# Where weight blocks and streamed tiles start in SBUF: bytes left free at the head of five pools

## The chip, the cores and the metric

The kernel runs on one core of a Trainium2 chip. The metric is the device time of one execution in microseconds; three runs of the kernel before took 2027.7, 2025.62 and 2027.94 us, a median of 2027.7.

## The reference, cut to what matters

Two transformer blocks over one sequence of 512 tokens, 1024 wide, in float32. The first block is a feed-forward layer, a mixer (attention of three kinds beside a state-space layer), a second feed-forward layer and a gate. The second block has two layers, each a recurrent branch beside an mLSTM branch, with a projection in and a projection out. Almost all of the arithmetic is in products of a weight matrix with the activations:

```python
def swiglu(x, w1, w3, w2):
    return (jax.nn.silu(x @ w1) * (x @ w3)) @ w2
...
    h = h + 0.5 * swiglu(rmsnorm(h, norm_ffn1[i]), ffn1_w1[i], ffn1_w3[i], ffn1_w2[i])
    z = rmsnorm(h, norm_mix[i]) @ w_in[i]
...
    h = h + jnp.concatenate([o_nsa, o_s5], axis=-1) @ w_out[i]
    h = h + 0.5 * swiglu(rmsnorm(h, norm_ffn2[i]), ffn2_w1[i], ffn2_w3[i], ffn2_w2[i])
    gate = jax.nn.sigmoid(rmsnorm(h, norm_ple[i]) @ w_ple_gate[i])
...
    for l in range(DEPTH_2):
        h = rms_norm(x, norm_g[l]) * (1.0 + scale[:, None, :]) + shift[:, None, :]
        u = h @ w_in[l]
...
        y = jnp.concatenate([y_rg, y_ml], axis=-1) @ w_out[l]
```

## The kernel before

**Tiling.** Activations lie feature-major: a tile is 128 features (the partitions) by 512 tokens, 2048 bytes in each partition. A weight matrix is cut into blocks of 128 x 128, 512 bytes in each partition. Both are split into two parts of type float32r, a high and a low one, and `mm3` (L111) makes a product of three instructions: high weights with the high tile (L115), high weights with the low tile (L116), low weights with the high tile (L117). In each the weight block is the operand that is loaded into TensorE beforehand, and the tile of 512 tokens is streamed past it. For one output tile `mm3` runs over all blocks of a column of the weight matrix and adds up in one PSUM bank; two banks (pa and pb in the tiles' names, followed by the stage) take turns.

**Weights.** `Stream` (L46) brings the blocks in the order of their use, eight to a chunk of 4096 bytes in each partition: one DMA into a tile of the pool `wst` (L71), a copy on ScalarE that makes the high part `whi` (L86) and a subtraction on VectorE that makes the low part `wlo` (L88). Two chunks are loaded and two split ahead of use.

**Streamed tiles.** xnh and xnl, the parts of a layer's normed input, lie in the pool `xp` of 26 tiles. gh and gl, the inputs of a feed-forward layer's second product, lie in the pool `ffn` that `swiglu` opens (L254); xch, rxh, yrh, ymh and their low parts in the pool of a layer of the second block (`layer`, L1400), apart from yrl, which lies in `xp`; oh, ol, sh, sl in `mix2`, some oh and ol in `xp`; pp, the gate's second input, in `ple`.

**Order.** The order of the instructions of each engine is the order in which the program issues them; nothing is rescheduled.

**Places.** A pool gets a stretch of every partition's bytes and lays its tiles one behind the other. The pools at the bottom (`const`, `wst`, `whi`, `wlo`, `work`, `xp`) stay for the whole program; those of the stages are opened and closed above them. The pool `const` ends at byte 20192, which is 224 past a multiple of 512, so all weight blocks and the tiles of `xp` begin at such places. A stage's pool begins wherever the one under it ends.

Of the kernel before, what the change touches and what calls it, by code (L numbers as in the profile page):

```python
# [44 lines left out]

class Stream:  # L46
    """Weight blocks of 128 x 128 in the order of their use, eight to a chunk, each chunk
    loaded ahead and split into two float32r parts."""
# [12 lines left out]
    def release(self):  # L61
        """Go on with the splits that were held back."""
        self.hold = False
        self.split(self.pos // CH + 1 + self.SPLIT)
# [34 lines left out]
    def get(self, *blocks):  # L99
        """The next blocks (name, slicer, row, column), side by side."""  # L100
        n = len(blocks)
        c, r = divmod(self.pos, CH)
        assert r + n <= CH
        self.split(c + 1 + (0 if self.hold else self.SPLIT if r >= CH // 2 else self.SPLIT - 1))
        self.order += list(blocks)
        self.pos += n
        s = slice(r * 128, (r + n) * 128)
        return self.hi[c][:, s], self.lo[c][:, s]


def mm3(k, ps, w, x, start, stop):  # L111
    """ps += (w_hi + w_lo).T @ (x_hi + x_lo), all but the product of the low parts,
    which lies under the last bit."""
    mm = k.nc.tensor.matmul
    mm(ps, w[0], x[0], start=start, stop=False)  # L115
    mm(ps, w[0], x[1], start=False, stop=False)  # L116
    mm(ps, w[1], x[0], start=False, stop=stop)  # L117


class Norm:  # L120
    """Sums of squares of a feature-major tensor, gathered tile by tile, and the reciprocal
    root in both layouts."""
# [7 lines left out]
    def add(self, src, scale=1.0):  # L130
        """Two sums, one to an engine, put together at the end; where the end is waited for,
        the last tile stays by itself."""
# [25 lines left out]
    def early(self, eps=1e-6):  # L158
        """The mean but for the last tile."""
        k = self.k  # L160
        self.head = k.work.tile([128, 4], F32, name="nhead", bufs=2)
        k.nc.vector.tensor_scalar(self.head, self.colsums(self.acc[0]), 1.0 / DM, eps, op0=OP.mult, op1=OP.add)
# [29 lines left out]
def rsqrt(k, out, ms):  # L192
    """out = ms ** -0.5 by Newton steps from the exponent's half."""
# [14 lines left out]
def split_scaled(k, src, g):  # L208
    """The two float32r parts of src * g (g one value to a partition)."""
# [19 lines left out]
class Fill:  # L229
    """Work to be laid into the gaps that the matrix products leave to the other engines."""  # L230
# [23 lines left out]
def swiglu(k, xs, norm, w1, w3, w2, parts, on_tile, rate, at):  # L254
    """h += 0.5 * swiglu of the input whose parts are xs; norm is still to be finished."""
    nc = k.nc
    f0 = 0
    with k.tc.tile_pool(name="ffn", bufs=2) as pool:
        for hf, n in enumerate(parts):
# [50 lines left out]
def sincos(k, pool, phi, shape, name, sign=1.0):  # L310
    """Sine (with a sign) and cosine of an angle of any size: steps to be run in order, and a dict that
    gets the tiles "s" and "c"."""
# [26 lines left out]
def s5_prepare(k, pool, ins, scr):  # L339
    """Steps that lay the state-space layer's matrices into DRAM scratch."""  # L340
# [255 lines left out]
def rope(k, ps, out, b, scale, done, todo):  # L596
    """The halves of each head changed over in b; the rest with the steps that follow."""
# [13 lines left out]
def gelu(k, y, out, w, todo=None):  # L611
    """Twice the tanh form, which the reference has; w is room to work in."""
# [24 lines left out]
def mixer(k, xs, norm, ins, scr, on_tile):  # L637
    nc, v = k.nc, k.nc.vector
    with ExitStack() as outer:
# [137 lines left out]
        def step(b):  # L777
            """The outputs of one block of groups."""
# [7 lines left out]
        def keys(b):  # L786
            """The keys of each group twice over the partitions, high parts; the low parts once."""
# [10 lines left out]
        # the compressed keys and values  # L798
        KV = {}

        def cmp_blocks(x):
            """The tokens of each block, by the parity of the token, with the positions added."""
# [48 lines left out]
        def cmp_k(g):  # L851
            """The keys of the two groups, each on its own partitions and columns."""
# [8 lines left out]
        def cmp_v(g):  # L861
            """The values under each of a tile's two heads of both groups, apart from the other's."""
# [12 lines left out]
        # the order of the projections  # L875
# [87 lines left out]
        p2 = outer.enter_context(k.tc.tile_pool(name="mix2", bufs=1))  # L963

        k.phase = "att"

        # the compressed branch's weights, all heads and tokens
# [48 lines left out]
        # the two branches that see every earlier token  # L1016
        oT, op, qs = {}, {}, {}

        def att_q(j):
            """The high parts of a head's queries and the low parts, on the partitions one above the other."""  # L1020
# [10 lines left out]
        def att_s(u, g):  # L1031
            """Scores and their weights."""
# [19 lines left out]
        def att_d(u, g):  # L1052
            """The gate over the weights' sum on a diagonal."""
# [8 lines left out]
        def put(u, g, ps, at, t, kb):  # L1062
            """The weights on the tokens of one tile of keys, scaled, with the keys on the partitions."""
# [39 lines left out]
        # the gate of the state-space layer  # L1103
# [46 lines left out]
def log1p_small(k, pool, e, out, shape, name):  # L1150
    """ln(1 + e) for 0 <= e <= 1: twice the inverse hyperbolic tangent of e / (2 + e)."""
# [13 lines left out]
def second_prepare(k, pool, ins):  # L1165
    """Steps: what the two later layers take from their vectors alone."""
# [13 lines left out]
    for l in range(2):  # L1180
# [34 lines left out]
        def colsum(n, L=L, box=box):  # L1215
            """Eight of the columns' sums."""
# [112 lines left out]
def modulate(k, l, norm, gg, scr):  # L1329
    """The parts of the layer's input, and the residual set aside."""  # L1330
# [28 lines left out]
def between(k, scr, nf, ng):  # L1359
    """The first block's closing norm and the second's first in one pass: with m the mean of the  # L1360
    squares before the closing norm and n the mean after its gain alone, the product of the two
    reciprocal roots is (n + eps (m + eps)) ** -0.5."""
# [37 lines left out]
def layer(k, l, xs, aside, ins, scr, norm):  # L1400
    """One layer of the second block: xs the parts of its scaled and shifted input, aside the
    steps that set its residual aside, norm the next one."""
    nc, v = k.nc, k.nc.vector
    L = k.lay[l]
    with ExitStack() as st:
        pool = st.enter_context(k.tc.tile_pool(name=f"lay{l}", bufs=1))
        NX = k.NX
# [21 lines left out]
        def pad(ps):  # L1429
            """The input with three tokens of zeros ahead of it."""  # L1430
# [5 lines left out]
        def conv(xp, w, b):  # L1436
            """Four taps over the tokens."""
# [9 lines left out]
        def silu2(ps, name):  # L1447
            """Twice the silu."""
# [7 lines left out]
        # mLSTM: inputs, queries, keys, values, gates  # L1456
# [4 lines left out]
        def gate_mm(w, x):  # L1461
            """Products in two parts go to the first rows, float32 ones to the others in turn."""
# [33 lines left out]
        def ml_in(ms):  # L1496
            """Convolution, silu (twice) and the parts, one tile a step behind the other."""
# [101 lines left out]
        def gates2():  # L1599
            """Each row twice, so that its high and its low part come to lie in one tile."""  # L1600
# [25 lines left out]
        # mLSTM: a head  # L1626
        H = {}

        def head_w(h):
            """The weights of the tokens for each other from the gates, keys on the partitions."""  # L1630
# [100 lines left out]
        def later(i, y, name):  # L1731
            """The high part now, the low part with the steps that follow."""
# [16 lines left out]
        # RG-LRU  # L1749
# [67 lines left out]
        # the steps in their order  # L1817
# [54 lines left out]
def vec_layout():  # L1872
    """Columns of the packed vectors: name -> (first column, columns)."""
# [16 lines left out]
def body(tc, ins, out, dbg):  # L1890
    nc = tc.nc
    with ExitStack() as ctx:
# [5 lines left out]
        k.wst = pool("wst", Stream.AHEAD + 1)  # L1898
        k.whi = pool("whi", Stream.SPLIT + 2)
# [71 lines left out]
        with tc.tile_pool(name="prep", bufs=1) as pp:  # L1971
            k.fill.steps += s5_prepare(k, pp, ins, scr)
            swiglu(k, xs, norm, "ffn1_w1", "ffn1_w3", "ffn1_w2", (6, 6, 5, 5), lambda d: feed("norm_mix", d), R1,
                   ((1, 0, 6), (1, 1, 4)))
# [10 lines left out]
        with tc.tile_pool(name="prep2", bufs=1) as pp:  # L1985
# [6 lines left out]
            with ple_p as lp:  # L1992
                def load_p():
# [5 lines left out]
                def split_p():  # L1999
                    for d in range(2):  # L2000
# [3 lines left out]
                       lambda d: feed("norm_ple", d), R2, ((0, 1, 5), (1, 0, 7)))  # L2004
# [35 lines left out]
def pack(inputs, order):  # L2040
    """The arrays that the program takes, laid out from the inputs."""
# [116 lines left out]
```

## Time and profile before

| | |
|---|---|
| median of three runs | 2027.7 us |
| lowest and highest | 2025.62, 2027.94 us |
| span of the profiled execution, first to last instruction | 2025.7 us |
| TensorE (PE) busy, share of the span | 1970.8 us, 97% |
| VectorE (DVE) busy, share | 1336.8 us, 66% |
| ScalarE (ACT) busy, share | 815.9 us, 40% |
| mean granted clock of TensorE, of full speed | 0.981 |

The profiled execution has no time of its own beside its span; the span lies within the scatter of the runs. PE is a product, PEld the loading of a weight block. Products are pipelined: one starts before the one ahead of it has ended, and the ends are modelled. The time of a run of products is therefore read from their starts: the first start, the last start, and the number of steps between.

### The profile page before, as it was taken

The numbers are of one execution on the slowest core, as the hardware profiler recorded it, in microseconds if no ns is written. First come the engines' busy times: TensorE is split into PE (matmuls) and PEld (weight loads), VectorE is DVE, ScalarE is ACT, GpSimd is POOL, SyncE is SP. The second block draws the span as 40 slices with busy tenths as digits, with TensorE's granted clock in tenths as the row PEclk, the third lists the DMA queues.
The fourth block names the chain that finished last, engine by engine and source line by source line (L and its number), as shares of the span: only waits on it lengthen the run. The fifth ranks groups of instructions, "written<-read, shape, count | busy, mean of one in ns | idle before, by whom it ended". The sixth has DMA issues, their size and how long they took to land. (4 is left out here: it accounts for less than half of the span.)

```text
span 2025.7 us, 24981 instructions
## 1 busy us (share of the span) xinstructions
PE 1970.8 (97%) x9432; PEld 1603.4 (79%) x9432; DVE 1336.8 (66%) x2241; ACT 815.9 (40%) x1227; POOL 159.9 (8%) x219
## 2 busy tenths in 40 slices
PE   8999999997999999999999999999999899999997
PEld 6888888886767888888888887887878677888885
DVE  7766576678655576667666675877752765777733
ACT  5323233436554332322244355554531444554521
POOL 1000000110242100000001100100000100001000
PEclk9999999998999999999999799999999899999998
DMA  5335545465201455365433143222232142232331
GB/s 186 101 114 155 159 129 152 159 192 160 89 8 35 151 182 195 117 222 167 166 104 94 47 141 115 78 89 74 83 136 94 62 156 94 73 94 84 95 124 52
DMA packets 100377, 239.59 MB, mean 118 GB/s; under 512 B 24600, under 2 KB 35608, under 8 KB 100256
## 3 DMA queue, kind: packets, MB, share of 16 engines
q1 hardware_dynamic: 100112, 237.82, 36.3%
q8 instruction: 74, 1.21, 0.3%
q14 instruction: 47, 0.39, 0.1%
q10 hardware_dynamic: 144, 0.17, 0.0%
HBM read 215.67 MB, written 21.10 MB: 117 GB/s over the span
## 5 line engine op out<-in xcount | busy, mean ns | idle before, releaser
L88 DVE TENSOR_TENSOR wlo<-wstage,whi 128x1024 fp32r<-128x1024 f32 (+1 forms) x305 | 377.3, 1244 | 150.3 <-ACT whi L86 146.8
L86 ACT ACTIVATE whi<-wstage 128x1024 fp32r<-128x1024 f32 (+1 forms) x306 | 313.4, 1043 | 144.9 <-DMA wstage<-in_wpack_dram 39.3
L266 ACT ACTIVATE t<-t 128x512 f32<-128x512 f32 x44 | 27.8, 632 | 176.3 <-DVE t L265 176.3
L1211 DVE SCALAR_TENSOR_TENSOR adaa<-adaw,b2c,adaa 128x256 f32<-128x256 f32 x168 | 81.3, 484 | 5.1
L117 PE MATMUL pahead<-xnh,wlo 128*128 128x512 f32 x208 | 81.3, 391 | 2.8 <-DVE wlo L88 2.8
L115 PE MATMUL pahead<-xnh,whi 128*128 128x512 f32 x208 | 83.4, 401 | 0.0
L143 POOL TENSOR_TENSOR nacc<-nacc,nsq 128x512 f32<-128x512 f32 x20 | 26.9, 1347 | 690.2 <-ACT nsq L139 690.2
L116 PE MATMUL pahead<-xnl,whi 128*128 128x512 f32 x208 | 81.0, 390 | 0.0
L115 PE MATMUL pbhead<-xnh,whi 128*128 128x512 f32 x192 | 77.5, 404 | 0.0
L115 PE MATMUL pbfirst<-xnh,whi 128*128 128x512 f32 x176 | 70.7, 402 | 6.8 <-ACT whi L86 6.5
L116 PE MATMUL pbhead<-xnl,whi 128*128 128x512 f32 x192 | 76.2, 397 | 0.0
L117 PE MATMUL pbhead<-xnh,wlo 128*128 128x512 f32 x192 | 75.9, 395 | 0.0
L1441 DVE SCALAR_TENSOR_TENSOR conv<-cpad,vec,conv 128x512 f32<-128x512 f32 x96 | 72.2, 752 | 5.6
L116 PE MATMUL pbfirst<-xnl,whi 128*128 128x512 f32 x176 | 69.8, 397 | 0.1
L117 PE MATMUL pbfirst<-xnh,wlo 128*128 128x512 f32 x176 | 69.5, 395 | 0.0
L115 PE MATMUL pasecond<-xnh,whi 128*128 128x512 f32 x176 | 69.1, 393 | 0.0
L115 PE MATMUL pbsecond<-xnh,whi 128*128 128x512 f32 x176 | 68.8, 391 | 0.0
L115 PE MATMUL pafirst<-xnh,whi 128*128 128x512 f32 x176 | 68.7, 390 | 0.0
L117 PE MATMUL pasecond<-xnh,wlo 128*128 128x512 f32 x176 | 68.6, 390 | 0.0
L117 PE MATMUL pafirst<-xnh,wlo 128*128 128x512 f32 x176 | 68.6, 390 | 0.0
L116 PE MATMUL pafirst<-xnl,whi 128*128 128x512 f32 x176 | 68.5, 389 | 0.0
L117 PE MATMUL pbsecond<-xnh,wlo 128*128 128x512 f32 x176 | 68.5, 389 | 0.0
(754 smaller groups left out, 5274.9 us busy)
## 6 DMA issues: line engine op xcount, KB each, us to landing
wstage<-in_wpack_dram SPq DMA_DIRECT2D x304, 512.0 KB, 3.8
adaw<-in_wada_dram SPq DMA_DIRECT2D x48, 512.0 KB, 4.8
scr_v<-vv SPq DMA_DIRECT2D x16, 256.0 KB, 2.1
vr<-scr_v SPq DMA_DIRECT2D x16, 256.0 KB, 4.2
xr<-scr_x SPq DMA_DIRECT2D x16, 256.0 KB, 5.5
h<-in_xT_dram SPq DMA_DIRECT2D x8, 256.0 KB, 5.6
s5vw<-scr_wq SPq DMA_DIRECT2D x64, 32.0 KB, 2.0
s5vb<-in_s5bq_dram SPq DMA_DIRECT2D x8, 256.0 KB, 2.7
```

What stands on the lines that cost most here:

```text
L86: k.nc.scalar.activation(hi[:, s], st[:, s], AF.Copy)
L88: eng.tensor_sub(lo[:, s], st[:, s], hi[:, s].bitcast(F32))
L115: mm(ps, w[0], x[0], start=start, stop=False)
L116: mm(ps, w[0], x[1], start=False, stop=False)
L117: mm(ps, w[1], x[0], start=False, stop=stop)
L143: k.nc.gpsimd.tensor_add(self.acc[1], self.acc[1], sq)
L266: nc.scalar.activation(t1, t1, AF.Silu)
L1211: v.scalar_tensor_tensor(a, w[:, d], cd, a, op0=OP.mult, op1=OP.add)
L1441: v.scalar_tensor_tensor(c, xp[:, 1 + j:1 + j + T], w(j), c, op0=OP.mult, op1=OP.add)
```

## The change

Five pools get a first tile named gap that nothing reads or writes, so that all tiles behind it in the pool begin later. The new function `room` makes it; `GAPS` holds the bytes in each partition. The gap at the head of `wst` (288 bytes) also moves everything above it. `swiglu` gets the name of its gap, which is 0 bytes for the second feed-forward layer. The rest of the diff takes comments and doc strings out, leaving empty lines.

```diff
+GAPS = {"base": 288, "ffn1": 320, "ffn2": 0, "lay": 320, "mix2": 224, "ple": 192}
+
+
+def room(pool, name):
+    if GAPS[name]:
+        pool.tile([128, GAPS[name] // 4], F32, name="gap", bufs=1)
...
-def swiglu(k, xs, norm, w1, w3, w2, parts, on_tile, rate, at):
+def swiglu(k, xs, norm, w1, w3, w2, parts, on_tile, rate, at, gap):
...
     with k.tc.tile_pool(name="ffn", bufs=2) as pool:
+        room(pool, gap)
...
         p2 = outer.enter_context(k.tc.tile_pool(name="mix2", bufs=1))
+        room(p2, "mix2")
...
         pool = st.enter_context(k.tc.tile_pool(name=f"lay{l}", bufs=1))
+        room(pool, "lay")
...
         k.wst = pool("wst", Stream.AHEAD + 1)
+        room(k.wst, "base")
...
-                   ((1, 0, 6), (1, 1, 4)))
+                   ((1, 0, 6), (1, 1, 4)), "ffn1")
...
             with ple_p as lp:
+                room(lp, "ple")
...
-                       lambda d: feed("norm_ple", d), R2, ((0, 1, 5), (1, 0, 7)))
+                       lambda d: feed("norm_ple", d), R2, ((0, 1, 5), (1, 0, 7)), "ffn2")
```

On every engine and in the DMA queue the same instructions stand in the same order with the same waits. Only addresses differ. Where tiles begin, in bytes past a multiple of 512, with the number of products of 512 columns by a full weight block that stream them:

| streamed tiles | products | tile before | weights before | tile now | weights now |
|---|---|---|---|---|---|
| xnh, xnl, yph, ypl, yrl, two of the oh and ol | 4736 | 224 | 224 | 0 | 0 |
| gh, gl of the first feed-forward layer; xch, xcl, rxh, rxl, yrh, ymh, yml | 1464 | 416 | 224 | 0 | 0 |
| gh, gl of the second feed-forward layer; pp | 576 | 32 | 224 | 0 | 0 |
| sh, sl, the other oh and ol | 144 | 0 | 224 | 0 | 0 |

Of the 4736, 128 stream yrl and 48 stream oh or ol, each between products that stream tiles of the other rows; 4560 stream xnh, xnl, yph and ypl. Eight of the 1464 belong to a small step outside `mm3`.

## Rows read from the trace of the kernel before

**Rows 1.** The page: span; busy us, share, instructions; costliest groups, mean ns behind busy us.

```profile
span 2025.7 us, 24981 instructions
...
PE 1970.8 (97%) x9432; PEld 1603.4 (79%) x9432; DVE 1336.8 (66%) x2241; ACT 815.9 (40%) x1227; POOL 159.9 (8%) x219
...
L88 DVE TENSOR_TENSOR wlo<-wstage,whi 128x1024 fp32r<-128x1024 f32 (+1 forms) x305 | 377.3, 1244 | 150.3 <-ACT whi L86 146.8
L86 ACT ACTIVATE whi<-wstage 128x1024 fp32r<-128x1024 f32 (+1 forms) x306 | 313.4, 1043 | 144.9 <-DMA wstage<-in_wpack_dram 39.3
```

**Rows 2.** Waits of TensorE, longest in total: us, times, longest.

```profile
PE pbfirst L115 <- ACT whi L86: 6.5, 1, 6.5
```

**Rows 3.** TensorE by stretch: length, busy us (products), granted clock, DMA share, GB/s.

```profile
282.00:288.00 6.00, 6.00 (x27) 1.00 0.20 47
...
315.00:320.00 5.00, 5.00 (x24) 1.00 0.03 11
...
1583.00:1589.00 6.00, 5.26 (x12) 0.50 0.12 20
```

**Rows 4.** Timeline of TensorE, clock at 0.50: start us, us, instruction, tiles.

```profile
1584.76 0.63 PE L115 MATMUL pbgates<-xnh,whi 128*128 128x512 f32 x1
...
1588.60 0.63 PE L115 MATMUL pagates<-xnh,whi 128*128 128x512 f32 x1
```

**Rows 5.** Timeline, first feed-forward layer, first products: 24 steps.

```profile
314.86 0.39 PE L115 MATMUL pbfirst<-xnh,whi 128*128 128x512 f32 x1
...
320.30 0.39 PE L115 MATMUL pafirst<-xnh,whi 128*128 128x512 f32 x1
```

**Rows 6.** Timeline, first feed-forward layer, second product: 24 steps.

```profile
281.74 0.40 PE L115 MATMUL pbfirst<-gh,whi 128*128 128x512 f32 x1
...
287.34 0.40 PE L115 MATMUL pafirst<-gh,whi 128*128 128x512 f32 x1
```

**Rows 7.** Timeline, second feed-forward layer, second product: 24 steps.

```profile
768.29 0.39 PE L115 MATMUL pbsecond<-gh,whi 128*128 128x512 f32 x1
...
773.79 0.39 PE L115 MATMUL pasecond<-gh,whi 128*128 128x512 f32 x1
```

**Rows 8.** Timeline, the mixer's output: 15 steps to the second row, 24 to the third.

```profile
659.86 0.40 PE L115 MATMUL pamixout<-sh,whi 128*128 128x512 f32 x1
...
663.36 0.39 PE L115 MATMUL pamixout<-oh,whi 128*128 128x512 f32 x1
...
665.45 0.40 PE L115 MATMUL pbmixout<-sh,whi 128*128 128x512 f32 x1
```

**Rows 9.** Timeline, output of a layer of the second block: 48 steps.

```profile
1481.77 0.39 PE L115 MATMUL paout<-yrh,whi 128*128 128x512 f32 x1
...
1492.98 0.39 PE L115 MATMUL pbout<-yrh,whi 128*128 128x512 f32 x1
```

**Rows 10.** Timeline, second projections inside a layer: 15 steps.

```profile
1244.96 0.40 PE L115 MATMUL pbgates<-xch,whi 128*128 128x512 f32 x1
...
1248.46 0.39 PE L115 MATMUL pagates<-xch,whi 128*128 128x512 f32 x1
```

**Rows 11.** Groups of TensorE by line and shape: count, busy us, mean ns.

```profile
L115 PE MATMUL pafirst<-gh,whi 128*128 128x512 f32 x88 | 35.0, 397 | 0.0
...
L115 PE MATMUL pbout<-ymh,whi 128*128 128x512 f32 x64 | 25.5, 399 | 0.0
...
L115 PE MATMUL pagates<-xch,whi 128*128 128x512 f32 x32 | 12.7, 397 | 0.0
...
L115 PE MATMUL pamixout<-sh,whi 128*128 128x512 f32 x16 | 6.7, 421 | 0.0
```

**Rows 12.** Groups of weight loads by line and shape: count, busy us, mean ns.

```profile
L115 PEld LDWEIGHTS pafirst<-xnh,whi 128*128 128x128 f32 x176 | 33.0, 188 | 7.1 <-issue 0.2
...
L115 PEld LDWEIGHTS pafirst<-gh,whi 128*128 128x128 f32 x88 | 16.5, 188 | 4.3 <-issue 0.4
```

**Rows 13.** One line on VectorE, both feed-forward layers: ns min/median/max, first and last start.

```profile
L225 DVE TENSOR_TENSOR gl<-t,gh x44: 691/693/695, 38.9 to 1042.9; 128x512 fp32r<-128x512 f32 x44
```

## The prediction

> **What bounds the kernel now.** I read the page's first part first. TensorE (PE) is busy 1970.8 of 2025.7 us, 97% of the span, and no other engine passes 66% [rows 1]. Then its waits: the longest, over the whole run, is 6.5 us and lies at the very start [rows 2]. So next to nothing is waited for; the time is the sum of TensorE's own products. The page's mean of one product (0.39 us) is no price, because products overlap and their ends are modelled. The price is the distance from one start to the next in the timeline, and the third reading is that distance, stage by stage, at the full granted clock.
>
> [...] The products that stream xnh and xnl start 24 in 5.44 us, **226.7 ns** each [rows 5]. The second product of the first feed-forward layer, the same instruction with the same weights' pools and only other tiles to stream, starts 24 in 5.60 us, **233.3 ns** [rows 6]. The second feed-forward layer: 24 in 5.50 us, 229.2 ns [rows 7]. The mixer's output: 24 in 5.59 us, 232.9 ns [rows 8]. The layers' output: 48 in 11.21 us, 233.5 ns [rows 9]. The layers' second projections (xch, xcl): 15 in 3.50 us, 233.3 ns [rows 10].
>
> What differs between these stages is where the streamed tile starts. The weights always start at 224 past a multiple of 512 bytes. xnh and xnl start at 224 too; gh and gl at 416 in the first feed-forward layer and at 32 in the second; xch, rxh, ymh at 416; sh and most of oh at 0. The fast stage is the only long one in which both operands start alike. That is a correlation in one trace, and two readings fit it: what counts is that both starts agree, or what counts is the streamed tile's own start, of which 224 happens to be the good one. They part here, since the change puts both at 0.
>
> **The change part by part.** It adds no instruction, moves none on any engine and alters no wait; its price is what the new places do.
>
> (a) *Streamed tiles that did not match the weights now do.* I price them at the pace of the one matched stage, 226.7 ns. The counts come from groups of 88, 64, 32 and 16 [rows 11], times their number. First feed-forward layer: 6 x 88 = 528 products x 6.6 ns = 3.5 us. Layers' output: 12 x 64 = 768 x 6.8 = 5.2 us. xch and rxh with their low parts: 6 x 32 + 6 x 16 = 288 x 6.6 = 1.9 us. Mixer's output: 12 x 16 = 192 x 6.2 = 1.2 us. Second feed-forward layer and the 48 products that stream pp: 576 x 2.5 = 1.4 us. Together 13.2 us. All of it lies on the engine that sets the end, so it comes off the time, unless the next thing is late. The weights' supply is not: eight blocks serve 24 products, 5.44 us at 226.7 ns, and the split of such a chunk takes ScalarE 1.04 and VectorE 1.24 us [rows 1]. Where the layers' gates and heads are worked out, TensorE goes in short stretches between the other engines' steps, and some of the 1.9 us may be lost there; I take **13.0 us**.
>
> (b) *The products that stream xnh, xnl, yph and ypl*, 4560 of them, matched at 224 before and matched at 0 now. This is the large unknown: 1 ns on each is 4.6 us. No row shows both operands at 0. From below it is bounded by the columns alone, 213.3 ns [rows 4]; from above by the nearest rows with the streamed tile at 0, sh and oh in the mixer's output, 15 in 3.50 us, 233.3 ns, though there the weights are at 224 [rows 8]. I take 226.7 ns, no change, because the rows nearest in kind are those in which the starts agree [rows 5]; the ends give -13.3 and +6.6 ns.
>
> (c) *Weight loads, splits, DMAs.* A weight load takes 188 ns whether the product beside it streams from 224 or from 416, and lies within the product before it [rows 12]. VectorE's 44 subtractions gl take 691 to 695 ns at both 416 and 32 [rows 13], so I give VectorE and ScalarE nothing for their new places. Of the weights' DMAs only the first is waited for, within the 6.5 us at the start [rows 2]. All this: 0, within 0.3 us either way.
>
> Sum: the profiled execution has a span of 2025.7 us, which becomes 2012.7. That span lies 2.0 us under the median of the runs, 2027.7, and inside their scatter. I carry the difference over: 2027.7 - 13.0 = **2014.7 us**.
>
> [...] The trace shows equal products at 226.7 and 233.3 ns with one clock [rows 3, 5, 6]. [...]
>
> **The rivals.**
>
> *Rival 1, aligned starts are cheaper in themselves.* [...] The 13.3 ns between 213.3 and 226.7 is one part in sixteen of the columns' time, as if 512 columns took the time of 544, and at 0 some of that would vanish. Half of it gone: the products of (a) and (b), 6912 of them, at 220.0 ns, another 6.7 x 6912 = 46 us, 1968.5 us. All of it gone: 1922 us. For it: a cause is needed for the 13.3 ns. Against it: tiles that start at 0 have no advantage in the mixer's output [rows 8].
> [...]
>
> *Rival 2, no change.* The paces belong to the stages and not to the places: to what else is running there, or to the order in which products follow one another (xnh, xnl, xnh is the same pattern everywhere, which speaks against it). Then the sum is 0: 2027.7, within 4 us.
>
> *Rival 3, slower.* The streamed tile's own start decides, and 0 is a bad one. The mechanism is that every product starts at the pace of sh and oh, 233.3 ns, wherever the weights are [rows 8]. The 4560 products of (b) lose 6.6 ns each, 30.1 us; the 576 of the second feed-forward layer and pp lose 4.1, 2.4 us; the others stay: 2027.7 + 32.5 = 2060.2 us. For it: 0 and 416 are equally bad. Against it: why 224 should be a good start by itself. It decides from a pace of 228.6 ns on: 13.2 us over 6912 products are 1.9 ns each, and 226.7 + 1.9 is the pace at which the gain of (a) is used up.
>
> **How the numbers follow.** Forecast 0.42, rival 1 0.23, rival 2 0.15, rival 3 0.20. The forecast's own range is 2010 to 2019: gates and edges may keep a quarter of the gain, and (b) may move by half a nanosecond. The range of all has to reach down over the half step of rival 1 (0.16 of its 0.23), over rival 2, and into the milder part of rival 3, where the pace is 230 ns or less: 1966 to 2042. A measurement of this kernel can tell about 0.2% from no change, 4 us. Faster than that: the forecast and rival 1, less a little of the forecast, 0.64; within it: 0.15; slower: 0.21.
>
> **What would show it.** In the profile of the changed kernel the starts of products that stream gh in both feed-forward layers and of ymh in the layers' output should lie 226.7 ns apart, and those of xnh too; TensorE's busy time and the span should both fall by about 13 us, and its waits stay as they are [rows 2]. A pace of 220 ns or less for xnh means rival 1; 233 ns for xnh means rival 3; gh still at 233.3 and 229.2 ns means rival 2. The forecast is wrong in its main step if xnh leaves 226.7 ns.

## The result, and the profile after

| | before | changed |
|---|---|---|
| median of five runs | 2027.42 us | 2015.1 us |
| lowest and highest | 2025.62, 2027.94 | 2013.55, 2015.33 |
| ratio of the times, 95% interval | | 0.9938 [0.9926, 0.995] |
| span of the profiled execution | 2025.7 us | 2011.8 us |
| TensorE busy | 1970.8 us | 1957.6 us |

The change takes 12.3 us off the median, 0.6%; the interval does not reach 1. The profiled execution of the changed kernel is the fastest of its five (2013.55 us), so its span flatters it by some 1.5 us against its own median. TensorE's busy time, 13.2 us less, comes from the same single execution; the medians are the measure. In each of the five runs the time is 1.7 to 1.8 us longer than the span (2013.55 and 2011.8 in the profiled one), so the 2.0 us between median and span before are mostly such an offset and not scatter.

The page of the changed kernel answers to [rows 1]: span; busy time, share and instructions; two groups of the weights' supply.

```profile
span 2011.8 us, 24981 instructions
...
PE 1957.6 (97%) x9432; PEld 1603.7 (80%) x9432; DVE 1335.3 (66%) x2241; ACT 815.5 (41%) x1227; POOL 161.7 (8%) x219
...
L98 DVE TENSOR_TENSOR wlo<-wstage,whi 128x1024 fp32r<-128x1024 f32 (+1 forms) x305 | 376.0, 1240 | 149.4 <-ACT whi L96 148.9
L96 ACT ACTIVATE whi<-wstage 128x1024 fp32r<-128x1024 f32 (+1 forms) x306 | 313.5, 1043 | 142.8 <-PE pasecond L126 36.1
```

Only PE's number moved by more than 2 us. The loads of weights (PEld), ScalarE, VectorE and GpSimd (POOL) are where they were, to 0.3, 0.4, 1.5 and 1.8 us.

The waits of TensorE after the change (us, times, longest) answer to [rows 2]:

```profile
PE pbfirst L125 <- ACT whi L96: 6.5, 1, 6.5
PE pbmix L125 <- DVE ropeo L613: 5.8, 1, 5.8
```

The first is the same wait at the start, 6.5 us. The second, for the rotated tile ropeo in the mixer, was 6.5 and is 5.8 us; the prediction named only the first of the two. The three waits for nacc, the sums of a norm, grew from 4.5 to 5.3 us together. No new wait has come.

Now the distance from start to start, in the timeline of TensorE after the change. Each pair of rows is the first and the last start of a run: 24 steps for xnh, gh of the first layer, the mixer's output and gh of the second layer, 15 steps for xch, 48 for the layers' output. They answer to [rows 5 to 10].

```profile
17.70 0.39 PE L125 MATMUL pafirst<-xnh,whi 128*128 128x512 f32 x1
...
23.14 0.39 PE L125 MATMUL pbfirst<-xnh,whi 128*128 128x512 f32 x1
...
81.83 0.39 PE L125 MATMUL pbfirst<-gh,whi 128*128 128x512 f32 x1
...
87.27 0.39 PE L125 MATMUL pafirst<-gh,whi 128*128 128x512 f32 x1
...
645.86 0.39 PE L125 MATMUL pamixout<-sh,whi 128*128 128x512 f32 x1
...
651.30 0.39 PE L125 MATMUL pbmixout<-sh,whi 128*128 128x512 f32 x1
...
764.96 0.39 PE L125 MATMUL pbsecond<-gh,whi 128*128 128x512 f32 x1
...
770.40 0.39 PE L125 MATMUL pbsecond<-gh,whi 128*128 128x512 f32 x1
...
1210.36 0.39 PE L125 MATMUL pagates<-xch,whi 128*128 128x512 f32 x1
...
1213.76 0.39 PE L125 MATMUL pbgates<-xch,whi 128*128 128x512 f32 x1
...
1474.52 0.39 PE L125 MATMUL paout<-yrh,whi 128*128 128x512 f32 x1
...
1485.39 0.39 PE L125 MATMUL pbout<-yrh,whi 128*128 128x512 f32 x1
```

All runs of 24 steps last 5.44 us, 226.7 ns a step; the layers' output 48 in 10.87 us, 226.5 (rows are rounded to 0.01 us, which is up to 0.2 ns a step here); xch 15 in 3.40, 226.7. Before, the same stages had 226.7, 233.3, 232.9, 229.2, 233.3 and 233.5. There is one pace left, and it is the one that xnh had all along.

To see that nothing else pays or is paid, I added up the distances from every product's start to the next start over the whole execution, by the tile that is streamed, in both traces (us):

| streamed tiles | products | before | after | difference | term of the prediction |
|---|---|---|---|---|---|
| gh, gl, first feed-forward layer | 528 | 124.08 | 120.87 | -3.21 | -3.5 |
| yrh, yrl, ymh, yml | 768 | 182.79 | 177.71 | -5.08 | -5.2 |
| xch, rxh and low parts | 288 | 68.38 | 66.97 | -1.41 | -1.9 |
| oh, ol, sh, sl (mixer's output) | 192 | 45.09 | 43.95 | -1.14 | -1.2 |
| gh, gl, second layer; pp | 576 | 132.63 | 131.35 | -1.28 | -1.4 |
| xnh, xnl, yph, ypl | 4560 | 1074.52 | 1073.30 | -1.22 | 0 |
| all other products | 2519 | 382.03 | 381.62 | -0.41 | 0 |
| together | 9431 | 2009.52 | 1995.77 | -13.75 | -13.0 |

The stages that were mismatched give 12.1 of the 13.75 us. Of the 1.2 us of xnh some 0.7 are the change's as well: before, a mismatched stage slowed the matched products behind it. The first rows are the first product of xnh behind the second feed-forward layer's gh and the one ten steps later, in the kernel before; the others are the same two in the changed kernel.

```profile
796.45 0.40 PE L115 MATMUL pasecond<-xnh,whi 128*128 128x512 f32 x1
...
798.76 0.39 PE L116 MATMUL pasecond<-xnl,whi 128*128 128x512 f32 x1
```

```profile
790.80 0.39 PE L125 MATMUL pasecond<-xnh,whi 128*128 128x512 f32 x1
...
793.07 0.39 PE L126 MATMUL pasecond<-xnl,whi 128*128 128x512 f32 x1
```

The ten steps take 2.31 us before and 2.27 after. Before, they are 234, 231, 234, 235, 225, 230, 236, 229, 232 and 231 ns long, and only then does the pace of 226.7 ns set in. There are fourteen such places in the kernel before, with five to ten slow steps each, and none in the changed kernel. So what a product costs depends on the products up to ten steps before it (225 to 236 ns a step in these ten, 226.7 further on), and the length of one step is not the price of one product.

What is left of the last two rows is of the size by which equal stages differ between executions: the mixer's wait is 0.7 us shorter, that for nacc 0.8 longer, and 48 instead of 55 of the 4560 products run at the lower clock (granted 0.50, 427 ns a step).

### The profile page after: what moved, and what is told of

Read it like the earlier page. It is cut to its first block, busy times and chain, and to the rows that moved or that the text cites. A ratio compares the mean times of both kernels' runs of the same rounds, so it can differ in the third digit from the quotient of the medians.

```text
span 2011.8 us, 24981 instructions
## 1 busy us (share of the span) xinstructions
PE 1957.6 (97%) x9432; PEld 1603.7 (80%) x9432; DVE 1335.3 (66%) x2241; ACT 815.5 (41%) x1227; POOL 161.7 (8%) x219
## 5 line engine op out<-in xcount | busy, mean ns | idle before, releaser
L98 DVE TENSOR_TENSOR wlo<-wstage,whi 128x1024 fp32r<-128x1024 f32 (+1 forms) x305 | 376.0, 1240 | 149.4 <-ACT whi L96 148.9
L96 ACT ACTIVATE whi<-wstage 128x1024 fp32r<-128x1024 f32 (+1 forms) x306 | 313.5, 1043 | 142.8 <-PE pasecond L126 36.1
L127 PE MATMUL pahead<-xnh,wlo 128*128 128x512 f32 x208 | 81.4, 391 | 2.8 <-DVE wlo L98 2.8
L126 PE MATMUL pahead<-xnl,whi 128*128 128x512 f32 x208 | 81.0, 390 | 0.0
L126 PE MATMUL pbhead<-xnl,whi 128*128 128x512 f32 x192 | 76.0, 396 | 0.0
L127 PE MATMUL pbhead<-xnh,wlo 128*128 128x512 f32 x192 | 76.0, 396 | 0.0
L126 PE MATMUL pbfirst<-xnl,whi 128*128 128x512 f32 x176 | 69.6, 395 | 0.3 <-DVE xnl L223 0.3
L127 PE MATMUL pbfirst<-xnh,wlo 128*128 128x512 f32 x176 | 69.1, 393 | 0.0
L127 PE MATMUL pafirst<-xnh,wlo 128*128 128x512 f32 x176 | 68.6, 390 | 0.0
L127 PE MATMUL pasecond<-xnh,wlo 128*128 128x512 f32 x176 | 68.6, 390 | 0.0
L126 PE MATMUL pafirst<-xnl,whi 128*128 128x512 f32 x176 | 68.5, 389 | 0.0
L127 PE MATMUL pbsecond<-xnh,wlo 128*128 128x512 f32 x176 | 68.5, 389 | 0.0
```

The costliest lines, as they stand in the source:

```text
L96: k.nc.scalar.activation(hi[:, s], st[:, s], AF.Copy)
L98: eng.tensor_sub(lo[:, s], st[:, s], hi[:, s].bitcast(F32))
```

## Experiments

**Which of the two does it: that the starts agree, or that they lie at multiples of 512?** Two kernels undo one half of the change each.

The first takes away the gap at the bottom:

```diff
-GAPS = {"base": 288, "ffn1": 320, "ffn2": 0, "lay": 320, "mix2": 224, "ple": 192}
+GAPS = {"base": 0, "ffn1": 320, "ffn2": 0, "lay": 320, "mix2": 224, "ple": 192}
```

> Only the gap at the bottom is taken away (base 288 -> 0). Weights and every streamed tile now start at 224 past a multiple of 512: they agree, and nothing lies at a multiple of 512. Theory A (what counts is that the streamed tile and the weight block start alike): 226.7 ns from start to start in every stage, 2015.1 us within 1.5, as fast as the changed kernel. Theory B (what counts is that the tiles lie at multiples of 512): gh stays at 233.3 and 229.2 ns as before, or everything is slower than 226.7, 2027 us or more.

Measured: 2015.85 us, ratio 0.9944 [0.9931, 0.9956]. The timeline, 24 steps of gh in the first feed-forward layer and 48 of the layers' output:

```profile
79.95 0.39 PE L125 MATMUL pbfirst<-gh,whi 128*128 128x512 f32 x1
...
85.39 0.39 PE L125 MATMUL pafirst<-gh,whi 128*128 128x512 f32 x1
...
1485.50 0.39 PE L125 MATMUL pbout<-yrh,whi 128*128 128x512 f32 x1
...
1496.38 0.39 PE L125 MATMUL paout<-yrh,whi 128*128 128x512 f32 x1
```

5.44 us for 24 steps and 10.88 for 48: 226.7 ns, with every operand 224 bytes past a multiple of 512. The whole gain is there without one tile at a multiple of 512.

The second leaves the gap at the bottom and takes away the others:

```diff
-GAPS = {"base": 288, "ffn1": 320, "ffn2": 0, "lay": 320, "mix2": 224, "ple": 192}
+GAPS = {"base": 288, "ffn1": 0, "ffn2": 0, "lay": 0, "mix2": 0, "ple": 0}
```

> Only the gap at the bottom is left (base 288, the four other gaps that differ from 0 taken away). Weights, xnh and xnl start at 0; gh of the first feed-forward layer and the layers' tiles at 192, gh of the second at 320, sh and oh at 288, so that each differs from the weights by as much as in the kernel before. Theory A (starts alike): the paces of the kernel before, 226.7 for xnh, 233.3 and 229.2 for gh in the first and the second layer, 233 for the outputs, and 2027.4 us within 1.5. Theory B (weights and xnh at multiples of 512 bring the gain): at least half of the 12.3 us is kept, 2021 us or less.

Measured: 2026.8 us, ratio 0.9999 [0.999, 1.0008]. 24 steps each of xnh, gh in the first and gh in the second layer:

```profile
16.16 0.39 PE L125 MATMUL pafirst<-xnh,whi 128*128 128x512 f32 x1
...
21.60 0.39 PE L125 MATMUL pbfirst<-xnh,whi 128*128 128x512 f32 x1
...
79.65 0.39 PE L125 MATMUL pbfirst<-gh,whi 128*128 128x512 f32 x1
...
85.25 0.39 PE L125 MATMUL pafirst<-gh,whi 128*128 128x512 f32 x1
...
766.85 0.39 PE L125 MATMUL pbsecond<-gh,whi 128*128 128x512 f32 x1
...
772.34 0.39 PE L125 MATMUL pasecond<-gh,whi 128*128 128x512 f32 x1
```

5.44, 5.60 and 5.49 us: the paces of the kernel before, 226.7, 233.3 and 228.8 ns, with the tiles at other places (192 and 320 instead of 416 and 32) but as far from the weights as before. Theory B is out in both directions. Between the places tried, 0 and 224 for the weights, the place itself makes no difference (226.7 ns at both where all agrees); the difference of the two starts decides.

**How well must they agree?** Three kernels, run once each, put the streamed tiles at other distances from the weights, which stay at 0. A gap at the head of the pool of xnh and xnl is new in all three; the first:

```diff
-GAPS = {"base": 288, "ffn1": 320, "ffn2": 0, "lay": 320, "mix2": 224, "ple": 192}
+GAPS = {"base": 288, "xp": 256, "ffn1": 192, "ple": 448, "ffn2": 64, "lay": 96, "mix2": 224}
...
+        room(k.xp, "xp")
```

> Weights at 0, the streamed tiles moved apart from them: xnh and xnl at 256, gh at 128 in the first feed-forward layer and at 64 in the second, the layers' tiles at 32, the mixer's output at 256, pp at 0. Theory A (the starts have to agree within 512 bytes): no stage is at 226.7 ns, all lie between 229 and 234; 4560 products of xnh at 229 to 233.3 and the others at their paces of before give 2025 to 2060 us. Theory A' (a smaller unit is enough, 256 or 128 or 64 bytes): xnh at 226.7 if 256 is a multiple of it, gh of the first layer too if 128 is, gh of the second too if 64 is, and the time stays near 2015 to 2023 us.

Measured: 2024.48 us, beside 2027.32 of the kernel before. 24 steps of xnh (256 from the weights) and 24 of gh in the first layer (128):

```profile
16.28 0.39 PE L125 MATMUL pafirst<-xnh,whi 128*128 128x512 f32 x1
...
21.72 0.39 PE L125 MATMUL pbfirst<-xnh,whi 128*128 128x512 f32 x1
...
81.16 0.39 PE L125 MATMUL pbfirst<-gh,whi 128*128 128x512 f32 x1
...
86.76 0.39 PE L125 MATMUL pafirst<-gh,whi 128*128 128x512 f32 x1
```

xnh at 256 is at 226.7 ns (5.44 us), which theory A did not allow and theory A' did for a unit of 256; gh at 128 is at 233.3. The time lies between the two theories' ranges. The two others:

```diff
+GAPS = {"base": 288, "xp": 384, "ffn1": 32, "ple": 320, "ffn2": 160, "lay": 160, "mix2": 480}
```

> As the run with xnh at 256, with other distances from the weights at 0: xnh and xnl at 384, gh at 96 in the first feed-forward layer and 160 in the second, the layers' tiles at 224, the mixer's output at 128. Theory A: all between 229 and 234 ns, 2025 to 2060 us. Theory A' (128 bytes are enough): xnh at 226.7 and the mixer's output too, the others slower, near 2027 us.

```diff
+GAPS = {"base": 288, "xp": 448, "ffn1": 352, "ple": 256, "ffn2": 416, "lay": 224, "mix2": 352}
```

> As the run with xnh at 256, with other distances from the weights at 0: xnh and xnl at 448 (or 64 bytes short of the weights), gh at 480 (32 short) in the first feed-forward layer and 416 in the second, the layers' tiles at 352, the mixer's output at 64. Theory A: all between 229 and 234 ns, 2025 to 2060 us. Theory A'' (what counts is how far the starts are apart, little hurts little): xnh at 448 and gh at 480 nearest to 226.7, the layers' tiles and gh at 416 farthest. A pace under 226.7 anywhere would say that agreeing starts are not the best.

Measured: 2046.48 and 2049.04 us. 24 steps of xnh at 384 in the one:

```profile
131.93 0.39 PE L125 MATMUL pbfirst<-xnh,whi 128*128 128x512 f32 x1
...
137.51 0.40 PE L125 MATMUL pafirst<-xnh,whi 128*128 128x512 f32 x1
```

and in the other 24 steps of xnh at 448 and of gh in the second layer at 416:

```profile
15.68 0.39 PE L125 MATMUL pafirst<-xnh,whi 128*128 128x512 f32 x1
...
21.28 0.39 PE L125 MATMUL pbfirst<-xnh,whi 128*128 128x512 f32 x1
...
775.80 0.40 PE L125 MATMUL pbsecond<-gh,whi 128*128 128x512 f32 x1
...
781.43 0.40 PE L125 MATMUL pasecond<-gh,whi 128*128 128x512 f32 x1
```

232.5, 233.3 and 234.6 ns; 128 bytes are not enough, so theory A' is out for that unit. With all stages of these three kernels, of the kernel before and of the kernel with the bottom gap alone, every distance in steps of 32 bytes is there at least once. The table has the mean distance of starts over a stage, steps of over 250 ns left out; of the outputs it counts only products whose whole step of three has that distance (ymh and yml, sh and sl):

| tile past the weights, bytes | 0 | 32 | 64 | 96 | 128 | 160 | 192 | 224 |
|---|---|---|---|---|---|---|---|---|
| ns | 226.9 | 233.5 | 229.1 | 233.3 | 233.3 | 234.3 | 233.3 | 233.0 |
| **and 256 more** | **256** | **288** | **320** | **352** | **384** | **416** | **448** | **480** |
| ns | 227.0 | 233.5 | 229.1 | 233.6 | 232.5 | 234.3 | 233.3 | 233.3 |

The second line repeats the first within 0.8 ns; two stages at one distance differ by as much as 1.0 (128 bytes: gh 233.3, sh and sl 232.3). So the pattern comes back every 256 bytes; only agreement to a multiple of 256 gives the pace of 226.7 ns (226.9 and 227.0 in the mean, with the irregular steps behind a wait), 64 bytes cost 2.2 ns, everything else 5.6 to 7.4. Being near does not help: 32 bytes on either side cost as much as 96 (theory A'' is out). No distance tried beats agreement.

For a product by itself agreement is not enough. The 48 products that stream pp lie at 0 with weights at 0 in all three kernels, between products of xnh. They have 226.8 ns where xnh lies at 256, but 230.0 and 230.2 where it lies at 384 and 448: the slow steps behind a mismatch again.

That 256 bytes are enough was then timed for the kernel as a whole. One gap more than in the change puts every streamed tile at 256, with the weights at 0:

```diff
-GAPS = {"base": 288, "ffn1": 320, "ffn2": 0, "lay": 320, "mix2": 224, "ple": 192}
+GAPS = {"base": 288, "xp": 256, "ffn1": 320, "ffn2": 0, "lay": 320, "mix2": 224, "ple": 192}
...
+        room(k.xp, "xp")
```

> The changed kernel with one more gap, 256 bytes at the head of the pool of xnh and xnl, which moves everything above it: weights at 0, every streamed tile at 256. Theory A256 (starts have to agree to a multiple of 256 bytes, as xnh at 256 suggests): 226.7 ns in every stage and 2015.1 us within 1.5. Theory A512 (only starts that agree to 512 bytes do; xnh at 256 had some other reason): gh and the outputs at 229 ns or more, 2020 us or more.

Measured: 2014.56 us, ratio 0.994 [0.9927, 0.9954]; 24 steps of gh in 5.44 us:

```profile
79.50 0.39 PE L125 MATMUL pbfirst<-gh,whi 128*128 128x512 f32 x1
...
84.94 0.39 PE L125 MATMUL pafirst<-gh,whi 128*128 128x512 f32 x1
```

Theory A256 holds. The ratio is that of the change, to the kernel before: it equals the change and does not beat it.

**With which block must the tile agree?** The load of the next product's block starts within 0.01 us of a product's start and takes 0.19 us of the 0.23 to the next start (the rows below). Is it that block or the product's own? Here the low weights alone were moved, to 320 (the gap of 192 behind them brings all that lies above back to 0):

```diff
-GAPS = {"base": 288, "ffn1": 320, "ffn2": 0, "lay": 320, "mix2": 224, "ple": 192}
+GAPS = {"base": 288, "ffn1": 320, "ffn2": 0, "lay": 320, "mix2": 224, "ple": 192, "wlo": 320, "xp": 192}
...
+        room(k.wlo, "wlo")
...
+        room(k.xp, "xp")
```

> The changed kernel with the blocks of the low weights wlo at 320 and everything else at 0. Of the three products of a step only the third (low weights with the high tile) has weights that start unlike its streamed tile; the block wlo is loaded while the second product (high weights with the low tile) streams. Theory A1 (a product is slowed by a block that is loaded beside it, and only if that block starts unlike the streamed tile): the distance from the second product's start to the third's grows from 226.7 to 233.3 ns, the two others stay. Theory A2 (a product is slowed by its own weights' place): the distance from the third's start to the next first one grows instead. Either way a third of the 6920 products loses 6.6 ns: 15 us, 2030 us. Theory A3 (an order of places that is not alike anywhere disturbs all three): all near 230 ns, 2038 us.

Measured: 2035.36 us (one run). First the order of things, in the timeline of this kernel: the second product (L126) and the third (L127), and the loads (PEld) that start beside them.

```profile
330.39 0.39 PE L126 MATMUL pbfirst<-xnl,whi 128*128 128x512 f32 x1
330.40 0.19 PEld L127 LDWEIGHTS pbfirst<-xnh,wlo 128*128 128x128 f32 x1
330.62 0.40 PE L127 MATMUL pbfirst<-xnh,wlo 128*128 128x512 f32 x1
330.63 0.19 PEld L125 LDWEIGHTS pbfirst<-xnh,whi 128*128 128x128 f32 x1
```

The block wlo is loaded beside the second product, and the next whi beside the third. The distances over the first layer's gh: 228.4 ns from the first product's start to the second's, 229.3 to the third's, 235.6 from the third's to the next first; mean 231.1. The long step is the third product's, as A2 said. But the two others grew as well, by 1.7 and 2.6 ns, which neither A1 nor A2 has, and the time is 5 us over the 2030 us of both. A3 comes nearest, all three near 230 ns and 2038 us, though it has no long step.

A record starts 0.4 us before its modelled end and only 0.23 us before the next start, so it may also be that what a mismatch costs shows late; that was tried for one step. The next kernel moved the low tiles gl in the first layer (to 192) and the high tiles gh in the second:

```diff
-GAPS = {"base": 288, "ffn1": 320, "ffn2": 0, "lay": 320, "mix2": 224, "ple": 192}
+GAPS = {"base": 288, "ffn1": 320, "ffn2": 192, "lay": 320, "mix2": 224, "ple": 192}
...
+            apart = {"ffn1": 192, "ffn2": 320}[gap] if hf == 0 else 0
...
-                gs.append(split_plain(k, pool, t2, "g", max(parts)))
+                gs.append(split_plain(k, pool, t2, "g", max(parts), apart))
...
-def split_plain(k, pool, src, name, bufs):
+def split_plain(k, pool, src, name, bufs, apart=0):
     hi = pool.tile([128, T], F32R, name=name + "h", bufs=bufs)
+    if apart:
+        pool.tile([128, apart // 4], F32, name="apart", bufs=1)
```

> The changed kernel, but in the first feed-forward layer the low tiles gl start at 192 (gh at 0) and in the second the high tiles gh at 192 (gl at 0); weights at 0. It asks with which block a streamed tile has to agree. Theory N (the block that is loaded beside it for the next product; what it costs shows one step later, as with the shifted low weights, where the step after the third product's start was the long one): first layer, the second product (gl) collides, and the step from the third product's start is long, 233 to 236 ns, the others 227 to 229; second layer, the first and third collide, and the steps from the second and the first product's start are long, that from the third short. Theory O (its own block, without delay): first layer, the step from the second product's start is long; second layer, those from the first and the third. Either way 2015.1 + 264/3 x 2 x 6.6 ns and twice that, some 3.5 us: 2018.6 us.

Measured: 2018.13 us (one run). First layer, steps from the first, second and third product's start: 229.5, 229.5, 228.3 ns, with no long one; second layer: 235.4, 237.5, 229.9, as theory N has it. One layer for N, one for neither; and since a mismatch slows steps up to ten products behind it, as the kernel before showed, single steps can't decide it. The last kernel tells the two apart by the mean of a stage: wlo and, in the first layer, gl both at 320, so that each streamed tile agrees with the block loaded beside it and two products in three disagree with their own.

```diff
+            apart = {"ffn1": 320, "ffn2": 0}[gap] if hf == 0 else 0
```

(with the GAPS line of the low weights' kernel, in which `ffn2` stays 0, and the other lines of the kernel above)

> As the kernel with the low weights wlo at 320 (whi, gh and xnh at 0), and in the first feed-forward layer the low tiles gl at 320 too; in the second layer gl stays at 0. In a step of three products, gl streams by high weights at 0 while the block wlo at 320 is loaded for the third, which streams gh at 0. Theory N (a streamed tile has to agree with the block that is loaded beside it for the next product, its own weights' place is nothing): in the first layer all three pairs agree, 226.7 ns although two of the three products have weights that start unlike their tile; in the second layer as with the shifted low weights, a mean of 231.1 ns. Theory O (with its own block): in the first layer two of the three products disagree, 231 to 234 ns, slower than or like the second layer. Time: 2035.4 us less 264 x 4.4 ns = 1.2 us by theory N (528 products, 4.4 ns each, are 2.3 us), 2035 or more by O; the paces decide, not the time.

Measured: 2039.27 us (one run). 24 steps of gh in the first layer:

```profile
82.14 0.40 PE L125 MATMUL pbfirst<-gh,whi 128*128 128x512 f32 x1
...
87.68 0.40 PE L125 MATMUL pafirst<-gh,whi 128*128 128x512 f32 x1
```

5.54 us, 230.8 ns; the stage's mean is 231.1, and the 528 products take 123.00 us from start to start, against 122.99 with gl at 0 and 120.87 where all is alike. Theory N, which had 226.7 ns here, is out. Theory O's range holds, but O did not name the long steps of the kernel ahead, and its sum doesn't come out: with the table's prices for each product's own block, 2.2 ns for gl (320 past whi) and 6.6 for the third product (its gh is 192 past wlo, modulo 512), it gives a mean of 229.6 ns here and 228.9 with gl at 0, and both were 231.1. So it stays open which two operands have to agree; what is shown is that only steps with all operands alike run at 226.7 ns. (That this kernel is 3.9 us behind the one with the low weights moved comes from the products of xnh, 1090.93 against 1086.70 us at the same pace of 231.1 ns within 0.1: 68 of them ran at the lower clock, granted 0.50, against 47, at 0.2 us more each.)

**What is left above 213.3 ns?** With the clock granted at 0.50 nine products start within 3.84 us [rows 3, 4], 426.7 ns each. Half of that, 213.3 ns, is an estimate of what 512 columns alone take at the full clock, if the whole distance goes with the clock; no stage ran at it. Rival 1 had to find a cause for the 13.3 ns that agreeing starts leave above it. First the load of the next block: in the feed-forward layers' second products the second and third product of each step but a sum's last took only 32 or 64 of the 128 weight columns.

```diff
-def mm3(k, ps, w, x, start, stop):
+def mm3(k, ps, w, x, start, stop, n=128):
...
+    n = 128 if stop else n
+    mm(ps[:n], w[0][:, :n], x[1], start=False, stop=False)
+    mm(ps[:n], w[1][:, :n], x[0], start=False, stop=stop)
...
+                    mm3(k, ps, k.ws.get((w2, f0 + i, m)), gs[i], i == 0, i == n - 1,
+                        32 if k.phase == "first" else 64)
```

> The changed kernel with everything at 0; in the second product of the feed-forward layers the second and the third product of a step take only 32 (first layer) or 64 (second layer) of the 128 weight columns, apart from the last step of a sum. The low parts of the other output features are left out of these sums. It asks where the 13.3 ns above 213.3 come from, which agreeing starts leave. [...] Theory A2 (a fixed cost of each product, whatever is loaded): 226.7 ns at either width.

Measured: 2018.09 us (one run). The weight loads by line and shape (count, busy us, mean ns), and 24 steps of gh in the first layer:

```profile
L125 PEld LDWEIGHTS pafirst<-gh,whi 128*128 128x128 f32 x88 | 16.5, 188 | 9.9 <-issue 0.4
...
L128 PEld LDWEIGHTS pasecond<-gh,wlo 128*64 128x64 f32 x72 | 9.7, 134 | 6.8
...
L128 PEld LDWEIGHTS pafirst<-gh,wlo 128*32 128x32 f32 x72 | 7.8, 108 | 8.8
```

```profile
81.58 0.39 PE L125 MATMUL pbfirst<-gh,whi 128*128 128x512 f32 x1
...
87.11 0.40 PE L125 MATMUL pafirst<-gh,whi 128*128 128x512 f32 x1
```

The loads are shorter, 134 and 108 ns instead of 188, and the products are no faster: 230.4 ns over these 24 steps, means over a layer's products of 230.5 (32 columns) and 229.5 (64). Less to load beside a product does not speed it up. A2's 226.7 is missed too; a stage of mixed widths is 3 to 4 ns a product slower, and why is open.

Second, whether the 13.3 ns belong to the product or to its columns: the feed-forward layers' second products, all steps of a sum but the first and last, streamed in two halves of 256 columns.

```diff
+    n = T // parts
+    for c in range(0, T, n):
+        c = slice(c, c + n)
+        mm(ps[:, c], w[0], x[0][:, c], start=start, stop=False)
+        mm(ps[:, c], w[0], x[1][:, c], start=False, stop=False)
+        mm(ps[:, c], w[1], x[0][:, c], start=False, stop=stop)
...
-                    mm3(k, ps, k.ws.get((w2, f0 + i, m)), gs[i], i == 0, i == n - 1)
+                    mm3(k, ps, k.ws.get((w2, f0 + i, m)), gs[i], i == 0, i == n - 1, 1 if i in (0, n - 1) else 2)
```

> The changed kernel; in the feed-forward layers' second product all steps of a sum but the first and the last stream their tiles in two halves of 256 columns: 672 products become 1344. It asks what the 13.3 ns are that a product takes beyond its columns' 213.3 where the starts agree. Theory C (one part in sixteen of the columns): a half takes 113.3 ns and the time stays at 2015. Theory F (a fixed cost of each product): a half takes 106.7 + 13.3 = 120 ns, 672 x 13.3 = 8.9 us more, 2024 us.

Measured: 2023.39 us (one run). The timeline, 23 steps of half products:

```profile
80.11 0.28 PE L128 MATMUL pbfirst<-gh,whi 128*128 128x256 f32 x1
...
82.86 0.28 PE L130 MATMUL pbfirst<-gh,wlo 128*128 128x256 f32 x1
```

2.75 us, 119.6 ns a half, where theory C wants 113.3 and theory F 120; the time is 8.3 us over the change's, F's 8.9. The products of 256 columns that the changed kernel has anyway (L1561 to L1563, 24 in a row) agree: 23 steps from 1187.50 to 1190.26 us, 120.0 ns each. From 256 columns to 512 the distance grows by 106.7 ns (120.0 to 226.7), which is half of the estimated 213.3. So between 256 and 512 columns the 13.3 ns are a cost of each product and do not grow with its columns. At 128 columns this no longer holds: products of 128 columns with a load each (L1702, type float32) start 112 ns apart in the changed kernel (ten steps from 1281.40 to 1282.52 us), where a quarter of 213.3 and 13.3 more would be 66.7. And in the kernel with halves the products left whole took 231.1 ns in the mean, 4.3 more than among their like, which is open as with the mixed widths. Products of more than 512 columns were not tried.

## Why the prediction was right

- **The reading of the trace.** "What counts is that both starts agree" against "the streamed tile's own start": the first, shown by the two kernels that undo half of the change. The correlation that the prediction had from one trace held, with one widening: agreement to 256 bytes is enough, and the prediction took 512 for granted. It says that most of oh lay at 0; half did. Its counts take in 176 products that matched already, yrl and that half of oh and ol; as they stand among mismatched ones and share their mean pace, the sum is not hurt.
- **The terms of (a).** 3.5, 5.2, 1.2 and 1.4 us came out as 3.21, 5.08, 1.14 and 1.28. Only xch and rxh gave clearly less, 1.41 of 1.9: their runs are short, 15 steps, and after each wait some steps are irregular until the pace sets in (mean of xch 227.7 ns, of rxh 228.2 instead of 226.7). The doubt of the prediction was put in the right place, but its 0.2 us were too little: 12.1 came of 13.2.
- **The term of (b).** In steady runs xnh stayed at 226.7 ns; no gain and no loss from the place 0 itself. Neither rival 1 (less than 226.7) nor rival 3 (233.3) shows in any stage. What the zero left out are the slow steps behind mismatched stages, 0.7 of the 1.22 us; the sum has no term for them.
- **Luck.** The terms of (a) were 1.1 us too high and the slow steps of (b), 0.7 us, were missing. The two errors go against each other, and the time came out nearer (2015.1 against 2014.7) than the terms did. The mechanism is not touched by that.
- **The term of (c).** The loads stay at 188 ns (the two groups of [rows 12]), and VectorE's gl takes 691, 693 and 695 ns as in [rows 13], now at 0. Zero holds.
- **The next thing that would be late.** The supply of weights, said not to be: the groups of wlo and whi take 1240 and 1043 ns, and no wait of TensorE for them has grown (the two longest, 6.5 us for whi and 2.8 for wlo, are as before).
- **Rival 2**, that the paces belong to the stages, falls with the same kernels: the same stage takes 226.7 or 233.3 ns by its place alone. One part of it is so: what ran just before a product counts for some ten steps (2.31 us for ten behind a mismatched stage, 2.27 behind a matched one).
- **What the places alone do.** The runs show equal products at 226.7, 229.1, 233.3 and 234.3 ns by nothing but the distance of two addresses (0 bytes in runs of 24 steps; 64, 192 and 160 in the table). Which two operands have to agree is open, and the kernel with narrower blocks shows that the amount loaded is not what counts: loads of 134 and 108 ns instead of 188, and products of 229.5 and 230.5 ns.
- **The 213.3 and 13.3 ns of (b) and rival 1.** No stage ran at 213.3 ns; it is half of the 426.7 ns at the clock of 0.50 [rows 3, 4], an estimate, and the 106.7 ns between 256 and 512 columns agree with it. The halves show 13.3 ns above it as a cost of each product of 256 or 512 columns with a load beside it (119.6 to 120.0 and 226.7 ns from start to start); at 512 columns it is the same at the place 0 as at 224.

13.0 us less were forecast: the medians of the times are 12.3 us apart, and in the two profiled executions, of which the changed kernel's is its fastest, the spans 13.9 and TensorE's busy times 13.2.

## What to carry to other kernels

Where one engine's products fill the span, read their price stage by stage as the distance from start to start; equal instructions with unequal prices may be a gain to be had. Let the tiles that TensorE streams and the blocks it loads start at the same place modulo 256 bytes: with the weights at 0 or at 224 the pace was the same, 226.7 ns a product, against 229.1 to 234.3 in the mean at the other distances tried, and a few hundred bytes left free at the head of a pool bring it about. This was tried with type float32r, blocks of 128 x 128 and a load for every product of 512 columns. Count the stages that already agree before pricing it; here two thirds of the products did, so 3% a product was 0.6% of the time. Read a pace well inside a stage, ten products or more behind its start: here five to ten steps behind a mismatched stage were slow.

## What the runs showed that was not expected

- Over the distances tried, 0 to 480 bytes, the cost of unlike starts has a period of 256 bytes and no slope in it: 5.6 to 7.4 ns on a product of 512 columns at every distance tried (steps of 32 bytes) but 0 and 64 (2.2 ns).
- The cost outlasts its cause: matched products behind a mismatched stage stay slow for five to ten steps (2.31 us instead of 2.27 for ten).
- Moving one of the four operands of a step slows all three of its products (low weights at 320: 1.7, 2.6 and 8.9 ns more). Moving gh alone, by 192, had a mean of 234.3 ns in the second layer, against 233.3 for gh and gl moved together in the first; but in the layers' output of the kernel before, yrh, 192 from the weights with yrl at none, has the same 233.5 as ymh and yml, both at 192.
- 13.3 ns stay on each product with a load beside it at 256 columns (119.6 ns) as at 512 (226.7), and a smaller block to load did not lessen them.
- Stages repeat to a few hundredths of a microsecond from kernel to kernel: the 528 products of gh take 120.87, 120.87 and 120.84 us in the three kernels whose starts agree, and 124.08 and 124.09 in two where they don't. What scatters between executions, by 2 to 4 us, is elsewhere; one part is how many products of xnh run at the lower clock, 47 to 70 in the thirteen traces, at 0.2 us more each.
